# A hybrid decoder trunk on one core: decay matrices from spread loads issued by GpSimd, the delta rule's made once and stored, convolutions in another place in memory

## The chip, the core and the metric

The kernel runs on one core of a Trainium2 chip. The core has TensorE (PE, matrix products, with a separate weight load that overlaps them), VectorE (DVE), ScalarE (ACT), GpSimd (POOL) and SyncE (SP). Each works off its own queue in order; semaphores hold one engine until another is done. DMAs can be issued from the queues of SP, ACT and POOL. On chip are SBUF (128 partitions) and PSUM (banks of 128 partitions x 512 float32, into which PE writes).

The metric is the time of one execution in microseconds (us), the median of several runs. Before the change it is 2346.28 us (three runs, 2346.13 to 2346.67).

## What is computed

Two layers of a trunk with 512 tokens of width 1024, all in float32. In each layer, one projection of the normalised input feeds three branches: an SSD branch (Mamba-2), latent attention (MLA), and a gated delta rule (GDN). Their outputs are gated, summed, projected, and followed by a feed-forward part. The change concerns the decay matrices of two branches. From the reference:

```python
# SSD: 2 groups of 8 heads, chunks of 128 tokens
A_cum = jnp.cumsum(A, axis=-1)
L = jnp.exp(jnp.where(tril, A_cum[..., :, None] - A_cum[..., None, :], -jnp.inf))
CB = jnp.einsum('bclgn,bcsgn->bcgls', Cc, Bc)
y_diag = jnp.einsum('bcgls,bgecls,bcsgep->bclgep', CB, L, X)
# delta rule: 8 heads
g = jnp.cumsum(chunks(g), axis=-1)
decay = jnp.exp(jnp.where(incl, g[..., :, None] - g[..., None, :], -jnp.inf))
a_mat = jnp.where(strict, jnp.einsum('bhcld,bhcmd->bhclm', kb, k) * decay, 0.0)
qk = jnp.where(incl, jnp.einsum('bhcld,bhcmd->bhclm', q, k) * decay, 0.0)
```

So for each head and each block of 128 tokens a matrix exp(c[l] - c[s]) is needed, where c is the running sum of the log decay in the block. There are 16 + 8 = 24 heads and 4 blocks (the reference takes the delta rule in chunks of 64, the kernel in blocks of 128; the output is mathematically the same). The delta rule uses its matrix twice: for the triangular matrix of keys against keys (`a_mat`), and for queries against keys (`qk`). Where l is before s the difference is positive; the kernel clips it at 0 before the exponential, and a mask takes that part away later.

## The kernel before

The kernel is written in a tile language: tiles come from pools, a tag names a set of buffers that its tiles take in turn, and a planner puts the instructions of each engine into an order at build time and sets the semaphores. The order in the source is the priority. So PE's queue holds matmuls of later parts of the source between those of a part that waits. Products in float32 accuracy are made of three products of split operands (`mm3`, L185): a weight tile `raw` is split into `hi` (ACT, L159) and `lo` (DVE, L160); four such pairs are kept (`wp`, 4 buffers of `whi` and `wlo`), and raw weights arrive by SP's DMAs (L166) into two buffers.

The order in each layer:

1. Small projections (64 rotary columns and the 32 columns of step sizes), then the query latent `cq`, the key latent `ck` (`latent`, L510), then four passes of two attention heads (L565 to L687). The pool `ml` holds the tiles of this part, the split latents (`cqh`, `cql`, `ckh`, `ckl`) among them. `step_sizes` (L402) runs after the first pass: it makes the log decays `g24` (128 tokens x 4 blocks x 24 heads), their sums by three matmuls with fixed matrices (`incl`, `gt`, `ones`, L431), and the exponentials of these (`dec`, L433).
2. `ml` is closed (L688) and the pool `br` for the other two branches is opened in the same memory (L709). Its tiles wait for the readers of what lay there.
3. `ssd_group(0)` (L1061): convolutions (`conv_silu`, L692: one ACT instruction and three DVE instructions into an accumulator `cva`, then a SiLU) on B, C (tiles `ft`) and X, the projection z, then four steps, one for each block of tokens t (L745). In each step two decay tiles `eE` of four heads (128 x 4 x 128) are made, multiplied by the masked product of C and B (L755), and used by PE as the left operand in eight products (L760).
4. Two of four parts of the attention's output projection (`out_proj`, L493), `ssd_group(1)`, and the other two parts.
5. `gdn_matrix` for each of two units of four heads (L812): keys, their products, and the triangular matrix `nt` with the decay tile (L845), written to memory (L849); `gdn_blocks` and `gdn_inverse` invert it between the rows of the SSD branch's output projection.
6. `gdn_unit` for the two units (L949): queries, values, z, then four steps with a decay tile each (L988 to L996, the product L1025), a power on POOL in each step (`rsq`, L269), then the branch's output projection.
7. Output projection, feed-forward.

How a decay tile is made before the change: `cum_rows` (L448), called once per layer in group 0 after z (L740), multiplies `g24`, laid out in 128 rows, with `incl` (four matmuls, L462), splits the result into high and low parts and builds from it, with constant selectors `sel` and `ind`, a left operand `W` and a right operand `M` (L464 to L476). `seg_exp` (L481) then takes the rows of four heads with `sel` (DVE, L484), makes all four difference matrices by one matmul of 128 x 512 into a PSUM bank (PE, L486), clips (ACT, L488) and takes the exponential (ACT, L489). It is called 16 times in the SSD groups, 8 times in `gdn_matrix` and 8 times in `gdn_unit`: 32 times per layer, 64 in all. The PSUM pool of these (`sm`) has three banks; `eE` has two buffers.

POOL does the powers (L271, L831, L961) and some memsets; no DMA is issued from its queue.

Of the kernel before, what the change touches and what calls it, by code (L numbers as in the profile page):

```python
# [29 lines left out]
NBLK = 6  # L30
# [6 lines left out]
def shape_constants():  # L37
# [7 lines left out]
    bmask = (k // 32 == np.arange(4)[None, :])  # L45
    r32 = k % 32
    sel = (r32 < 24) & (r32 // 4 == np.arange(6)[None, :])
    ind = (r32 < 24) & (r32 % 4 == np.arange(4)[None, :])
    pad = np.zeros((P, P - 14))
# [5 lines left out]
    mats = [ident, incl, gt, ones, nstrict, bmask, sel, ind, pad, neg, full, invc, sgn]  # L55
# [4 lines left out]
def hybrid_kernel(ctx, tc, a, out, depth=2, taps=None):  # L60
# [4 lines left out]
    def mk(pl, shape, dt, tag, bufs=None):  # L65
        return pl.tile(shape, dt, tag=tag, name=f"{tag}_{next(uid)}", bufs=bufs)
# [30 lines left out]
    def sm_bank():  # L97
        return mk(ps_sm, [P, 512], F32, "sm")
# [4 lines left out]
    ct = mk(cst, [P, NBLK * P + 80], F32, "ct")  # L103
# [6 lines left out]
    bmask, sel, ind = (ct[:, 5 * P + i : 5 * P + j] for i, j in ((0, 4), (4, 10), (10, 14)))  # L110
# [249 lines left out]
    for ly in range(depth):  # L360
# [40 lines left out]

        def step_sizes():  # L402
# [43 lines left out]
            return dec, ndec, beta, dtq, dsk, g24  # L446

        def cum_rows(pl):  # L448

            g4 = mk(pl, [P, T, 4, 32], F32, "wk0")
            pool.memset(g4.rearrange("p t a n -> p (t a n)"), 0.0)
            g2 = g24.unsqueeze(2).to_broadcast([P, T, 2, 24])
            dve.tensor_copy(g4[:, :, 0:2, 0:24], g2)
            dve.tensor_scalar(g4[:, :, 2:4, 0:24], g2, -1.0, None, ALU.mult)
            ps = sm_bank()  # L460
            for t in range(T):
                pe.matmul(ps[:, t * P : (t + 1) * P], g4[:, t].rearrange("p a n -> p (a n)"), incl, start=True, stop=True)  # L462
            hi = mk(pl, [P, S], F32R, "wk1")
            act.copy(hi, ps)  # L464
            lo = mk(pl, [P, S], F32R, "wk2")
            dve.tensor_tensor(lo, ps, f32(hi), ALU.subtract)
            W = mk(pl, [P, T, P], F32R, "cw")
            M = mk(pl, [P, T, 4, P], F32R, "cm")
            dve.tensor_copy(W[:64].rearrange("p t m -> p (t m)"), ones[:64, 0:1].to_broadcast([64, S]))
            i4 = ind.unsqueeze(2).to_broadcast([P, 4, P])  # L470
            for q, x in ((0, hi), (32, lo)):
                act.copy(W[64 + q : 96 + q].rearrange("p t m -> p (t m)"), f32(x[64 + q : 96 + q]))
                for t in range(T):
                    dve.tensor_tensor(M[q : q + 32, t], bc_mid(f32(x[q : q + 32, t * P : (t + 1) * P]), 4), i4[q : q + 32], ALU.mult)
            for t in range(T):
                act.copy(M[64:, t], i4[64:])  # L476
            return W, M

        cum = []

        def seg_exp(pl, o, t, h0):  # L481

            w = mk(pl, [P, P], F32R, "sg", 2)
            dve.tensor_scalar(w, f32(cum[0][:, t]), sel[:, h0 // 4 : h0 // 4 + 1], None, ALU.mult)  # L484
            ps = sm_bank()
            pe.matmul(ps, w, cum[1][:, t].rearrange("p i l -> p (i l)"), start=True, stop=True)  # L486
            of = o.rearrange("p i l -> p (i l)")
            act.activation(of, ps, AF.Relu, scale=-1.0)  # L488
            act.activation(of, of, AF.Exp, scale=-1.0)  # L489
# [20 lines left out]
        def latent(tok, width, gi, nm):  # L510
# [10 lines left out]
            hs, ls = hilo_tags(ml, nm, nk)  # L521
# [9 lines left out]
        cqh, cql = latent(cq_tok, 512, g_q, "cq")  # L531
        ckh, ckl = latent(ck_tok, 256, g_kv, "ck")
# [32 lines left out]
        for hp in range(4):  # L565
# [120 lines left out]
            if hp == 0:  # L686
                dec, ndec, beta, dtq, dsk, g24 = step_sizes()  # L687
# [4 lines left out]
        def conv_silu(pl, ps, taps_, bias, o):  # L692

            acc = mk(pl, [P, S], F32, "cva", 2)
# [17 lines left out]
        def ssd_group(g, yh, yl):  # L712
# [3 lines left out]
            bt = mk(br, [P, S], F32, "ft", 6)  # L716
            ctl = mk(br, [P, S], F32, "ft", 6)
            btok = mk(br, [P, T, P], F32, "kt", 2)

            def conv(ps, c, o):  # L720
                conv_silu(br, ps, [sconv(j, c) for j in range(4)], col(sconv_b + c), o)
# [17 lines left out]
            if g == 0:  # L739
                cum[:] = cum_rows(br)  # L740
# [61 lines left out]
        def gconv_silu(ps, c, o):  # L802
            conv_silu(br, ps, [gconv(j, c) for j in range(4)], None, o)

        def key_tiles(c0):
# [4 lines left out]
            return res  # L810

        def gdn_matrix(u):  # L812
# [136 lines left out]
        def gdn_unit(u, kT, ork, cc, cd, Yt, yh, yl):  # L949
# [35 lines left out]
            for t in range(T):  # L985
                tok = slice(t * P, (t + 1) * P)
                Y = Yt[:, t]
                e = mk(br, [P, 4, P], F32, "eE", 2)  # L988
                seg_exp(br, e, t, hd0)
# [320 lines left out]
```

## Time and profile before

| | |
|---|---|
| median of three runs | 2346.28 us (2346.13 to 2346.67) |
| the profiled execution's own time | 2345.51 us |
| its span, first to last instruction | 2343.7 us |
| granted clock of PE, mean | 0.999 |
| bytes read from and written to device memory | 200.50 MB, 7.34 MB |
| decay matmuls (L486) | 64 |

The profile is of one execution. PE is the matmul side of TensorE, PEld its weight load. A line such as L486 is a line of the kernel before. A group of the profile reads: line, engine, operation, output tile <- input tiles, shape, count, then busy time in us and the mean of one in ns, then the idle time of that engine just before these instructions and what ended most of it. Matmuls are pipelined, so the duration of one is longer than the distance to the next. The chain of waits is followed back from the last instruction to what released each; its rows give a start, a duration and the instruction, and where PE splits a product into several instructions, each is counted.

### The profile page before, as it was taken

What the parts mean: (1) busy time and instruction counts of PE and PEld (TensorE: products, weight loads), DVE (VectorE), ACT (ScalarE), POOL (GpSimd) and SP (SyncE); (2) the same over time, 40 slices, a digit from 0 to 9 for tenths busy, and PEclk for the clock granted to TensorE, in tenths of its full rate; (3) what the DMA queues carried; (4) which work ended last, traced back from release to release, by engine and by line L of the source; (5) the groups of instructions that cost most, each with busy time, mean ns of one, the idle gap of its engine ahead of it and who ended that gap; (6) DMA issues with size and microseconds to landing.
All of it is one profiled execution on the core that took longest, in us unless ns stands there. A gap on an engine that the chain in (4) does not pass through costs nothing.

```text
span 2343.7 us, 32132 instructions
## 1 busy us (share of the span) xinstructions
PE 2310.1 (99%) x12004; PEld 1898.8 (81%) x12004; DVE 1608.3 (69%) x3186; ACT 1153.3 (49%) x2303; POOL 58.3 (2%) x76
## 2 busy tenths in 40 slices
PE   8999999999999999999999999999999999999998
PEld 7787788888887888888888887888887878888886
DVE  6776857775665458767767776667756645677668
ACT  6665434533544345544656553444335534555545
POOL 0000000000000000000000000000000000000000
PEclk9999999999999999999999999999999999999999
DMA  4222222252222442233132222223422124332231
GB/s 137 86 72 66 71 90 72 77 149 73 72 66 70 144 153 101 72 125 117 44 102 79 73 73 72 90 72 99 118 81 72 59 77 156 132 114 102 90 108 45
DMA packets 194173, 215.16 MB, mean 92 GB/s; under 512 B 32353, under 2 KB 153697, under 8 KB 194017
## 3 DMA queue, kind: packets, MB, share of 16 engines
q1 hardware_dynamic: 190496, 207.87, 27.9%
q10 hardware_dynamic: 3520, 5.25, 0.9%
q8 instruction: 94, 1.54, 0.3%
q14 instruction: 63, 0.51, 0.1%
HBM read 200.50 MB, written 7.34 MB: 89 GB/s over the span
## 4 chain that ended last, share of the span: by engine, by line
PE 90%; DVE 5%; ACT 1%; DMA 1%; POOL 1%; issue 1%; SPq 0%; DVEq 0%; POOLq 0%; ACTq 0%
PE acc L187 23%; PE acc L188 23%; PE acc L189 23%; PE sm L187 2%; PE sm L188 2%; PE sm L189 2%; PE sm L760 1%; DVE wlo L160 1%; PE sm L664 1%; PE yt L188 1%; PE sm L1025 1%; PE yt L187 1%; PE yt L189 1%; PE sm L486 1%; PE sm L1006 1%
## 5 line engine op out<-in xcount | busy, mean ns | idle before, releaser
L160 DVE TENSOR_TENSOR wlo<-wraw,whi 128x512 fp32r<-128x512 f32 x552 | 378.1, 688 | 399.7 <-ACT whi L159 389.8
L159 ACT CAST whi<-wraw 128x512 fp32r<-128x512 f32 x552 | 341.9, 621 | 621.0 <-PE acc L188 408.1
L187 PE MATMUL acc<-xh,whi 128*128 128x512 f32 (+1 forms) x1184 | 462.1, 391 | 0.0
L188 PE MATMUL acc<-xl,whi 128*128 128x512 f32 (+1 forms) x1184 | 459.4, 388 | 0.0
L189 PE MATMUL acc<-xh,wlo 128*128 128x512 f32 (+1 forms) x1184 | 459.0, 388 | 0.0
L188 PEld LDWEIGHTS acc<-xl,whi 128*128 128x128 f32 x1184 | 223.0, 188 | 42.3 <-issue 1.0
L189 PEld LDWEIGHTS acc<-xh,wlo 128*128 128x128 f32 x1184 | 222.9, 188 | 42.1 <-issue 0.5
L187 PEld LDWEIGHTS acc<-xh,whi 128*128 128x128 f32 x1184 | 222.8, 189 | 41.7 <-issue 0.5
L187 PE MATMUL acc<-yh,whi 128*128 128x512 f32 x384 | 153.0, 402 | 0.0
L188 PE MATMUL acc<-yl,whi 128*128 128x512 f32 x384 | 152.4, 397 | 0.0
L189 PE MATMUL acc<-yh,wlo 128*128 128x512 f32 x384 | 151.3, 394 | 0.0
L189 PE MATMUL acc<-whi,xl 128*128 128x512 f32 (+1 forms) x384 | 143.8, 375 | 0.0
L187 PE MATMUL acc<-whi,xh 128*128 128x512 f32 (+1 forms) x384 | 143.6, 376 | 0.0
L188 PE MATMUL acc<-wlo,xh 128*128 128x512 f32 (+1 forms) x384 | 143.2, 373 | 0.0
L701 DVE SCALAR_TENSOR_TENSOR cva<-acc,pc,cva 128x511 f32<-128x511 f32 (+2 forms) x168 | 120.2, 743 | 16.8 <-ACT cva L697 9.5
L159 ACT CAST whi<-wr 128x512 fp32r<-128x512 f32 x128 | 79.5, 621 | 68.2 <-PE acc L189 31.9
L189 PE MATMUL acc<-whi,yl 128*128 128x512 f32 x256 | 99.7, 389 | 0.0
L187 PE MATMUL acc<-whi,yh 128*128 128x512 f32 x256 | 99.7, 389 | 0.0
L188 PE MATMUL acc<-wlo,yh 128*128 128x512 f32 x256 | 99.6, 389 | 0.0
L160 DVE TENSOR_TENSOR wlo<-wr,whi 128x512 fp32r<-128x512 f32 x128 | 85.9, 686 | 12.5 <-ACT whi L159 11.7
L187 PEld LDWEIGHTS acc<-yh,whi 128*128 128x128 f32 x384 | 71.6, 188 | 16.8 <-ACT yh L266 2.3
L188 PEld LDWEIGHTS acc<-yl,whi 128*128 128x128 f32 x384 | 72.2, 188 | 16.0 <-issue 1.9
(413 smaller groups left out, 4603.1 us busy)
## 6 DMA issues: line engine op xcount, KB each, us to landing
wraw<-in_w_in_dram SPq DMA_DIRECT2D x148, 512.0 KB, 3.4
wraw<-in_w_up_dram SPq DMA_DIRECT2D x64, 512.0 KB, 3.6
wr<-in_w_down_dram SPq DMA_DIRECT2D x32, 1024.0 KB, 5.0
wraw<-in_w_mla_out_dram SPq DMA_DIRECT2D x16, 512.0 KB, 3.3
wraw<-in_w_ssd_out_dram SPq DMA_DIRECT2D x16, 512.0 KB, 3.4
wraw<-in_w_gdn_out_dram SPq DMA_DIRECT2D x16, 512.0 KB, 3.3
wraw<-in_w_out_dram SPq DMA_DIRECT2D x16, 512.0 KB, 3.6
wraw<-in_mla_w_uq_dram SPq DMA_DIRECT2D x16, 384.0 KB, 3.2
```

The source lines that it names most:

```text
L159: act.copy(hi, raw)
L160: dve.tensor_tensor(lo, raw, f32(hi), ALU.subtract)
L187: pe.matmul(o, ah, bh, start=start, stop=False, skip_group_check=more)
L188: pe.matmul(o, ah, bl, start=False, stop=False, skip_group_check=more)
L189: pe.matmul(o, al, bh, start=False, stop=stop, skip_group_check=more)
L486: pe.matmul(ps, w, cum[1][:, t].rearrange("p i l -> p (i l)"), start=True, stop=True)
L664: pe.transpose(ps[:, n : n + P], pn[t][:, kb * P : (kb + 1) * P], ident)
L701: dve.scalar_tensor_tensor(acc[:, d:], ps[:, : S - d], taps_[3 - d], acc[:, d:], ALU.mult, ALU.add)
L760: pe.matmul(py[:, h * 64 : (h + 1) * 64], e2[h // 4][:, h % 4, :], xd[:, h * 64 : (h + 1) * 64], start=True, stop=True)
L1006: pe.matmul(pw[:, h * P : (h + 1) * P], Y[:, h, :], r[:, h * P : (h + 1) * P], start=True, stop=True)
L1025: pe.matmul(po[:, h * P : (h + 1) * P], pt_[:, h, :], vn[:, h * P : (h + 1) * P], start=True, stop=True)
```

## The change

- The running sums are taken from the first of the three matmuls that `step_sizes` makes anyway (with `incl`): DVE copies 96 columns to a tile `cum`, PE transposes it, ACT copies the result, and SP's queue stores the rows to device memory (`d_c`: 4 blocks x 24 heads x 128 tokens).
- `seg_exp` becomes: a DMA issued from POOL's queue loads the rows of four heads and spreads them to all 128 partitions (2 KB to each, 256 KB); four ACT instructions, one for each head, subtract a column of `cum` and clip; one ACT instruction takes the exponential. No matmul, no DVE instruction and no PSUM bank is used.
- `cum_rows`, its tiles (`cw`, `cm`, `sg`, and its use of `wk0` to `wk2`) and the constants `bmask`, `sel`, `ind` go.
- The delta rule's eight decay tiles are made once, in a new function `gdn_decays` that is called right after `ssd_group(0)`, and stored by POOL's queue to device memory (`d_e`, 256 KB each). `gdn_matrix` and `gdn_unit` load them back by POOL's queue. So decay tiles are made 24 times per layer (16 + 8) and loaded back 16 times.
- `eE` has four buffers.
- The key latent's split tiles (`ckh`, `ckl`) move from the pool `ml` to `lp`, which stays open. The convolutions' accumulators take the place of `ckl0` and `ckl1` (before: two buffers `cva` in `br`, shared with `out_proj`), and the first group's B and C the place of `ckh0` and `ckh1`.
- The scratch memory for software-issued DMAs is set to 8192 bytes.

```diff
-NBLK = 6
+NBLK = 5
...
-    mats = [ident, incl, gt, ones, nstrict, bmask, sel, ind, pad, neg, full, invc, sgn]
+    mats = [ident, incl, gt, ones, nstrict, neg, full, invc, sgn]
...
+        cum = mk(sp, [P, T, 24], F32, "cum")
+        d_c = mk(dr, [T, 24 * P], F32, "d_c", 2)
...
+            dve.tensor_copy(cum.rearrange("p t n -> p (t n)"), ps[:, :96])
+            pc_ = sm_bank()
+            pe.transpose(pc_[:96, :P], cum.rearrange("p t n -> p (t n)"), ident)
+            rows = mk(ml, [96, P], F32, "crow")
+            act.copy(rows, pc_[:96, :P])
+            sync.dma_start(d_c.rearrange("t (n l) -> (t n) l", l=P), rows)
...
-        def cum_rows(pl):
...
-        def seg_exp(pl, o, t, h0):
-
-            w = mk(pl, [P, P], F32R, "sg", 2)
-            dve.tensor_scalar(w, f32(cum[0][:, t]), sel[:, h0 // 4 : h0 // 4 + 1], None, ALU.mult)
-            ps = sm_bank()
-            pe.matmul(ps, w, cum[1][:, t].rearrange("p i l -> p (i l)"), start=True, stop=True)
+        def seg_exp(o, t, h0):
+
             of = o.rearrange("p i l -> p (i l)")
-            act.activation(of, ps, AF.Relu, scale=-1.0)
+            pool.dma_start(of, d_c[t, h0 * P : (h0 + 4) * P].partition_broadcast(P))
+            for i in range(4):
+                act.activation(o[:, i], o[:, i], AF.Relu, scale=-1.0, bias=cum[:, t, h0 + i : h0 + i + 1])
             act.activation(of, of, AF.Exp, scale=-1.0)
...
-        cqh, cql = latent(cq_tok, 512, g_q, "cq")
-        ckh, ckl = latent(ck_tok, 256, g_kv, "ck")
+        cqh, cql = latent(ml, cq_tok, 512, g_q, "cq")
+        ckh, ckl = latent(lp, ck_tok, 256, g_kv, "ck")
...
-            acc = mk(pl, [P, S], F32, "cva", 2)
+            acc = mk(lp, [P, S], F32, f"ckl{next(convs) % 2}")
...
-            bt = mk(br, [P, S], F32, "ft", 6)
-            ctl = mk(br, [P, S], F32, "ft", 6)
+            bt, ctl = (mk(br, [P, S], F32, "ft", 6) if g else mk(lp, [P, S], F32, f"ckh{i}") for i in range(2))
...
-            if g == 0:
-                cum[:] = cum_rows(br)
...
-                e2 = [mk(br, [P, 4, P], F32, "eE", 2) for _ in range(2)]
+                e2 = [mk(br, [P, 4, P], F32, "eE", 4) for _ in range(2)]
                 for q in range(2):
-                    seg_exp(br, e2[q], t, h0 + 4 * q)
+                    seg_exp(e2[q], t, h0 + 4 * q)
...
+        def gdn_decays():
+
+            for u in range(2):
+                for t in range(T):
+                    e = mk(br, [P, 4, P], F32, "eE", 4)
+                    seg_exp(e, t, 16 + 4 * u)
+                    pool.dma_start(d_e[u, t], e)
...
-                e = mk(br, [P, 4, P], F32, "eE", 2)
-                seg_exp(br, e, t, hd0)
+                e = mk(br, [P, 4, P], F32, "eE", 4)
+                pool.dma_start(e, d_e[u, t])
...
+        d_e = mk(dr, [2, T, P, 4, P], F32, "d_e", 2)
         ssd_group(0, *ys)
+        gdn_decays()
         out_proj(a["w_mla_out"][ly], 1, *y_mla, br, (0, 1))
...
-    nc = bacc.Bacc("TRN2", target_bir_lowering=False, num_devices=1)
+    nc = bacc.Bacc("TRN2", target_bir_lowering=False, num_devices=1, dynamic_dma_scratch_size=8192)
```

The replaced call of `seg_exp` by a load stands in two places, `gdn_matrix` and `gdn_unit`.

More of the change, by code (lines that the diff above doesn't have):

```diff
@@ L445, in step_sizes @@
             tap("beta", beta)
[L446 to L486 removed]
+            return dec, ndec, beta, dtq, dsk
+        def seg_exp(o, t, h0):
             of = o.rearrange("p i l -> p (i l)")
[L488 removed]
+            pool.dma_start(of, d_c[t, h0 * P : (h0 + 4) * P].partition_broadcast(P))
+            for i in range(4):
+                act.activation(o[:, i], o[:, i], AF.Relu, scale=-1.0, bias=cum[:, t, h0 + i : h0 + i + 1])
             act.activation(of, of, AF.Exp, scale=-1.0)
@@ L507, in out_proj, with latent @@
                         dve.tensor_tensor(mixed[d], mixed[d], tg[j], ALU.add)
-        def latent(tok, width, gi, nm):
+        def latent(pl, tok, width, gi, nm):
             nk = width // P
@@ L802, in gconv_silu @@
         def gconv_silu(ps, c, o):
-            conv_silu(br, ps, [gconv(j, c) for j in range(4)], None, o)
+            conv_silu(ps, [gconv(j, c) for j in range(4)], None, o)
         def key_tiles(c0):
@@ L987, in gdn_unit @@
                 Y = Yt[:, t]
[L988 to L989 removed]
+                e = mk(br, [P, 4, P], F32, "eE", 4)
+                pool.dma_start(e, d_e[u, t])
                 pg = sm_bank()
```

17 lines of the change are left out of this document (6 added, 11 removed).

## The prediction

> **What bounds the kernel now.** I read the page's busy times first, then the shares of the chain of waits, then the table by stage, and last the groups of single lines.
>
> ```profile
> span 2343.7 us, 32132 instructions
> PE 2310.1 (99%) x12004; PEld 1898.8 (81%) x12004; DVE 1608.3 (69%) x3186; ACT 1153.3 (49%) x2303; POOL 58.3 (2%) x76
> ...
> PE 90%; DVE 5%; ACT 1%; DMA 1%; POOL 1%; issue 1%; SPq 0%; DVEq 0%; POOLq 0%; ACTq 0%
> ```
>
> TensorE (PE) is busy 99% of the span and makes up 90% of the chain that ended last; only 33.6 us of the span (2343.7 - 2310.1) has no matmul in it. GpSimd (POOL) does almost nothing. But a busy PE may be one that waits with a matmul open, so I looked at the stages that the change touches. In layer 0 they are: group 0 of the SSD branch, the time from there to group 1, group 1, the delta rule's matrices, the delta rule's two units. Columns: stretch, its length, then busy time of PE, weight load, DVE, ACT, POOL, granted clock, DMA share, GB/s.
>
> ```profile
> 236.00:284.00 48.00, 47.13 (x234) 37.12 (x232) 42.66 (x79) 22.22 (x44) 1.02 (x1) 1.00 0.19 57
> 284.00:358.00 74.00, 73.67 (x335) 60.30 (x336) 40.72 (x63) 30.23 (x50) 0.00 (x0) 1.00 0.30 92
> 358.00:395.00 37.00, 37.00 (x187) 29.17 (x186) 30.50 (x59) 16.90 (x35) 1.01 (x1) 1.00 0.19 58
> 432.00:470.00 38.00, 37.13 (x179) 30.31 (x178) 34.14 (x118) 20.53 (x36) 5.31 (x6) 1.00 0.30 86
> 600.00:732.00 132.00, 129.73 (x667) 105.27 (x666) 91.12 (x242) 67.90 (x176) 10.07 (x9) 1.00 0.19 60
> ```
>
> PE stands still for 0.87 us in group 0, for nothing in group 1, for 0.87 us at the matrices and 2.27 us in the units. The clock is full. VectorE (DVE) is the second engine everywhere: 89% in group 0 (42.66 of 48) and 90% at the matrices. ScalarE (ACT) is half idle. So a matmul that is taken out should shorten the kernel by the distance between two matmuls, as long as DVE's chain does not become the pace.
>
> **What is removed from PE.** The decay matrices are made by one matmul each (L486), on rows that `cum_rows` makes by four matmuls in each layer (L462).
>
> ```profile
> L486 PE MATMUL sm<-cm,sg 128*128 128x512 f32 x64 | 26.5, 445 | 0.6 <-DVE sg L484 0.6
> ...
> 170.33 0.39 PE L187 MATMUL acc<-xh,whi 128*128 128x512 f32 x1
> ...
> 171.01 0.39 PE L187 MATMUL acc<-xh,whi 128*128 128x512 f32 x1
> ...
> 237.08 0.89 PE sm L462 x8
> ...
> 1396.78 0.89 PE sm L462 x8
> ```
>
> The 445 ns of an L486 is its latency in a pipeline. Its price is the distance of starts: the two L187 rows, from a dense stretch, are three matmuls of the same width apart, 0.68 us, so 0.227 us each. 64 x 0.227 = 14.5 us. The chain has L462 with 0.89 us in each layer, 1.8 us together. Added on PE is one 96-column transpose per layer; eight narrow matmuls take 0.89, so 0.11 each, 0.2 us. Net: 14.5 + 1.8 - 0.2 = 16.1 us.
>
> Not all of it must count. 16 of the 64 L486 stand in the units (4 steps, 2 units, 2 layers), where PE already has its longest waits. If the recurrence sets the pace there, those 16 x 0.227 = 3.6 us come back as waiting. Between 0 and 3.6 I take the middle, 1.8: PE is idle in that stage for only 2% of the time, but the chain passes through GpSimd's and DVE's small steps there. Gain so far: 16.1 - 1.8 = 14.3 us.
>
> **DVE and ACT.** All are off the bound; these are their sums.
>
> ```profile
> L484 DVE TENSOR_SCALAR sg<-cw,ct 128x128 fp32r<-128x128 f32 x64 | 18.3, 300 | 10.0 <-PE sm L486 10.0
> L474 DVE TENSOR_TENSOR cm<-wk,ct 32x512 fp32r<-32x512 f32 x16 | 10.2, 675 | 0.1
> ...
> L489 ACT ACTIVATE eE<-eE 128x512 f32<-128x512 f32 x64 | 39.2, 630 | 0.7
> L488 ACT ACTIVATE eE<-sm 128x512 f32<-128x512 f32 x64 | 37.0, 595 | 45.5 <-PE sm L486 34.2 <-DVE tok L845 11.3
> ...
> L476 ACT CAST cm<-ct 64x512 fp32r<-64x512 f32 x8 | 4.5, 612 | 0.1
> ...
> 609.47 1.14 ACT L1013 ACTIVATE wk<-sm,gcd 128x128 f32<-128x128 f32 x4 [0.73 <-DVE wk L1008]
> ```
>
> DVE loses L484 and L474, 28.5 us, and gains one small copy per layer. DVE also loses a wait of 10.0 us for L486. That helps group 0 most: two L484 out of each step and eight L474 ahead of the first. I count no gain for it, because PE is full there; the bounds are 0 and, in both layers, the still time of the first three and the fourth rows above, 2 x (0.87 + 0.33 + 0 + 0.87) = 4.1 us. On ACT a clip becomes four instructions of 128x128 with a column as bias. The nearest row is L1013, four of 128x128 with a column as scale in 1.14 us. Matrices are made 48 times and no longer 64, for the delta rule's are stored and loaded twice. Out go 37.0 + 39.2 + 4.5 = 80.7 us, in come 48 x (1.14 + 0.63) = 85.0 us: 4 us more on an engine that is idle half the time. Where it is dense, behind group 0, eight matrices are added: 8 x 1.77 = 14.2 us on 30.23 of 74. It fits.
>
> **The DMAs.** New are 48 spread loads, 16 stores and 32 loads back, all 256 KB and all on POOL's queue, and two small stores of the sums on SP's. No POOL DMA runs in the trace, so its price has to be bounded from other queues.
>
> ```profile
> L831 POOL TENSOR_TENSOR gork<-gss,phalf 128x8 f32<-128x8 f32 x4 | 6.6, 1638 | 130.9 <-DVE gss L829 130.9
> ...
> qh<-in_positions_dram SPq DMA_DIRECT2D x1, 256.0 KB, 4.9
> ...
> wk<-d_x SPq DMA_DIRECT2D x4, 256.0 KB, 5.0
> ...
> L166 SPq DMA_DIRECT2D wraw<-in_w_in_dram x148: 367/368/433, 4.5 to 1927.5; - x148
> ...
> L876 SPq DMA_DIRECT2D wk<-d_x x4: 371/1468/3038, 511.9 to 1672.0; - x4
> ```
>
> The load of the positions has exactly the new form, one 2 KB row spread over 128 partitions: 4.9 us from issue to landing. POOL's time for an issue lies between SP's usual 0.37 us and the longest issue of an L876, 3.04 us; I take 1.6, POOL's longest own calculation (L831), since the engine does such work in software steps. 96 x 1.6 = 154 us on an engine with 2285 us to spare. By bytes, 96 x 0.26 = 25 MB on 215: a twelfth more on queues that are busy 28%.
>
> Whether a load is late depends on the steps. Rows: the first products with a decay matrix in group 0, the last ones there, the first ones of group 1.
>
> ```profile
> 249.45 1.01 PE sm L760 x8
> ...
> 275.99 1.73 PE sm L760 x16
> ...
> 282.74 1.03 POOL srs L271
> ...
> 360.13 1.08 PE sm L760 x8
> ...
> L433 ACT ACTIVATE dec<-sm x2: 417/417/417, 105.0 to 1266.0; 128x288 f32<-128x288 f32 x2
> ```
>
> The sums are there at L433, 105 us, 144 us ahead of 249. SP's new store stands in front of weight loads in its queue and waits for one ACT copy at that time; I count nothing, and 2 x 0.6 us if that copy is behind another. Steps 0 and 1 of a group find their four buffers filled early. Between groups 20 issues (8 loads, 8 stores, 4 loads) have 360 - 276 = 84 us: hidden up to 4.2 us each. Steps 2 and 3 are the tight ones: a buffer is free after the products of the step two before, and a step is (275.99 - 249.45) / 3 = 8.8 us, so two steps less the products and the mask give about 14 us. Needed are two issues, 4.9 us, and two clips with exponentials, 3.5 us. Hidden up to (14 - 8.4) / 2 = 2.8 us per issue. With 1.6 nothing is exposed; with 3.04 it is 2 x 0.24 us for each of 8 pairs of loads (2 steps, 2 groups, 2 layers), 4 us.
>
> Behind a waiting load stand POOL's powers (L271). The group's is at 282.74 and its result is used a whole projection later. In unit 0 a load for unit 1 is free to go at the same step's last product, and the power comes after the copy, DVE and ACT work that follow that product. Behind a waiting clip stand ACT's weight casts.
>
> ```profile
> L159 ACT CAST whi<-wraw 128x512 fp32r<-128x512 f32 x552 | 341.9, 621 | 621.0 <-PE acc L188 408.1 <-PE acc L189 122.3 <-PE sm L188 25.0
> ...
> L895 ACT COPY tok<-wk 32x512 f32<-32x512 f32 x4 | 2.5, 617 | 5.5 <-DMA wk<-d_x 5.5
> ```
>
> The casts sit idle because PE has not yet freed a buffer (408.1 of 621.0 us): they run ahead. A pair of buffers feeds 12 matmuls, 2.7 us; three pairs in reserve cover 8.2 us.
>
> [...]
>
> **Convolution in the latent's place.** The first convolutions no longer need memory that attention frees.
>
> ```profile
> 180.00:190.00 10.00, 10.00 (x60) 7.95 (x59) 6.47 (x18) 5.00 (x14) 0.53 (x1) 1.00 0.17 52
> 190.00:200.00 10.00, 9.99 (x52) 8.06 (x51) 7.43 (x14) 7.52 (x15) 0.00 (x0) 1.00 0.16 52
> ```
>
> PE does not stop at that passage (10.00 and 9.99 of 10), so it is worth nothing; its cover is PE's other queued matmuls, and with less of these it could be worth the few tenths that stand idle there. Smaller constants and scratch cost no time.
>
> **Sum.** The profiled span is 2343.7 us and its run 2345.51, against a median of 2346.28: 2.6 us lie between span and median. 2343.7 - 14.3 + 2.6 = 2332.0 us. With the bounds (0 or 3.6 lost in the units, 4.1 won from still time, 4 + 1.2 lost to issues and SP) the forecast's own range is 2326 to 2339.
>
> **Rivals.**
> (a) The engines behind PE set the pace. For: DVE at 89 to 90% in group 0 and the matrices. Against: PE idles under 1 us there, and DVE is relieved too. Then the 32 matmuls in the groups and the 16 in the units give nothing, 48 x 0.227 = 10.9, of which 1.8 is counted: 2332 + 9.1 = 2341.
> (b) The loads of steps 2 and 3 come late and hold ACT, whose order is fixed, and so PE's products behind it: the one place where the change adds a short wait. For: L895 is such a wait of ACT for a load from memory, 5.5 us in two layers, 2.75 each. Against: 5.6 us of slack for each pair. At 2.75 for each of the 8 pairs: 22 us, 2354. It decides from 14.3 / 8 = 1.8 us per pair. If an issue held POOL for the whole 5.0 us, a pair would lose 2 x 2.2 us, 35 us, 2367.
> (c) More than the matmuls is won: three PSUM banks no longer shared with the decay matrices, ACT no longer waiting 34.2 us for L486 and DVE 10.0 us. For: these rows. Against: no idle PE to win it from. If the still time of the touched stages, units too, 2 x 4.34 = 8.7 us, went: 2332 - 8.7 = 2323.
>
> **From this to the numbers.** Forecast 0.58, (a) 0.12, (b) 0.20, (c) 0.10. This kernel's runs spread by 0.02%, and I call 0.2%, 4.7 us, the least that can be told from no change: faster is under 2341.6, slower over 2351.0. Faster: forecast, (c), and half of (a), 0.74. Same: the rest of (a) and 0.04 of (b), 0.10. Slower: 0.16. The range goes from 2320, under (c), to 2354, (b) at L895's price; outside are about 0.10 above and 0.03 below.
>
> **What will show it.** Right: PE's count of 128x512 matmuls falls by 64 and L462 is gone, while PE stays at 99%; the clips wait for no load in steps 2 and 3; POOL's issues take under 2.8 us. Wrong: ACT's new clip line with waits for loads of 2 us and more, followed by PE waiting in the L760 line; POOL's power in the units starting late behind a load; or PE's share falling below 98% at 236 to 284 and 600 to 732 with DVE nearly full, which would be (a).

## The result and the profile after

The changed kernel takes 2352.71 us (median of 19 runs, 2344.45 to 2358.88), the kernel before 2347.03 on the same chip (19 runs, 2346.13 to 2349.86): a ratio of 1.0024, 95% interval [1.0017, 1.0031]. It is 5.7 us slower, where 14.3 us less was forecast. The runs of before lie within 4 us, those of after within 14. The profiled execution of after is the slowest of them, 2358.88 us, so the traces differ by more than the medians: 13.4 us of span. Line numbers are those of each kernel, so the same code stands at a lower number in after.

The head of the page of after, and its chain of waits:

```profile
span 2357.1 us, 32210 instructions
...
PE 2305.1 (98%) x11926; PEld 1898.6 (81%) x11926; DVE 1582.6 (67%) x3100; ACT 1159.7 (49%) x2403; POOL 112.2 (5%) x170
...
PE 80%; issue 6%; DVE 6%; DMA 4%; ACT 2%; POOL 1%; SPq 0%; ACTq 0%; POOLq 0%; DVEq 0%
```

The matmuls are gone (78 records fewer), yet PE is busy only 5.0 us less, and the time without a matmul rose from 33.6 to 52.0 us. In the chain DMA rose from 1% to 4%, and "issue", time in which an engine waits for nothing that the profile shows, from 1% to 6%. Where PE stands still is shown by the waits of PE, and why by the waits of ACT (waiting tile and line, what it waited for, us in total, times, longest):

```profile
PE sm L730 <- DVE eE L725: 10.0, 6, 2.1
PE sm L879 <- DMA wk<-d_x: 5.9, 2, 3.7
...
ACT eE L457 <- DMA eE<-d_c: 39.7, 20, 5.0
```

L730 are the products with a decay matrix in the ssd groups (L760 before), L725 the mask on that matrix, L879 the first products of the delta rule's inverse (L901 before, where this wait was 0.9 us). Before has no wait over 0.3 us at these products or at the matmuls that make their matrices. The same shows by stage, in columns as in the prediction's table:

```profile
232.00:280.00 48.00, 43.15 (x215) 33.62 (x214) 34.40 (x60) 28.47 (x72) 9.44 (x17) 1.00 0.43 132
280.00:354.00 74.00, 73.99 (x336) 60.80 (x335) 37.12 (x55) 39.07 (x78) 4.81 (x9) 1.00 0.44 129
354.00:395.00 41.00, 38.91 (x190) 30.50 (x189) 30.87 (x53) 18.78 (x44) 4.68 (x9) 0.96 0.37 115
...
600.00:740.00 140.00, 136.75 (x704) 112.04 (x703) 92.48 (x240) 61.87 (x164) 13.41 (x13) 1.00 0.26 73
```

In group 0, PE is idle for 4.85 us of 48 (0.87 before), though DVE fell from 89% to 72% and ACT is at 59%: no engine is full, so something is late. In group 1 the granted clock is 0.96 and no longer full. What is late in group 0 is seen in the timelines of POOL, ACT, DVE and PE (start, duration, engine, line; in brackets the idle time ahead and what ended it):

```profile
240.90 0.55 POOL L455 DMA_DIRECT2D eE<-d_c  x1 [43.31 <-DVE wlo L154]
242.65 0.55 POOL L455 DMA_DIRECT2D eE<-d_c  x1 [1.20 <-ACT st L747]
...
248.10 0.55 POOL L455 DMA_DIRECT2D eE<-d_c  x1 [0.34 <-ACT eE L458]
...
244.58 0.40 ACT L457 ACTIVATE eE<-eE,cum 128x128 f32<-128x128 f32 x1 [2.67 <-DMA eE<-d_c]
...
248.71 0.63 ACT L458 ACTIVATE eE<-eE 128x512 f32<-128x512 f32 x1
...
253.35 0.40 ACT L457 ACTIVATE eE<-eE,cum 128x128 f32<-128x128 f32 x1 [0.59 <-DMA eE<-d_c]
...
254.81 0.69 DVE L154 TENSOR_TENSOR wlo<-wraw,whi 128x512 fp32r<-128x512 f32 x1 [2.40 <-ACT whi L153]
...
256.25 0.96 PE L730 MATMUL sm<-wk,eE 128*128 128x64 f32 x7 [1.88 <-DVE eE L725]
```

POOL starts the loads of step 2 at 240.90 and 242.65, when the products of step 0 have freed their buffers. ACT, in its fixed order, stands at the clips until they land. But step 2's matrix is finished in time: its second exponential (248.71) ends at 249.34, and PE comes to its products at 254.37 (256.25 less the 1.88 of waiting). What is late is its mask, and the chain of waits ahead of these products shows by what:

```profile
248.10 5.14 DMA eE<-d_c
...
253.35 0.07 ACT eE L457
...
253.66 0.61 ACT eE L458
254.27 0.52 ACT whi L153
...
254.81 0.04 DVE wlo L154
...
255.42 0.70 DVE eE L725
...
256.25 1.09 PE sm L730 x8
```

The load of 248.10 belongs to step 3. ACT stands at its clip; behind the clip, in ACT's order, stands a weight cast (L153); for that cast DVE stands 2.40 us at the weight's low part (L154); and behind L154, in DVE's order, stands the mask of step 2. At step 3's products, where PE waits another 1.88 us until 267.40, the same chain begins at the first loads for the delta rule, issued at 257.86 and 258.75. Right ahead of the mask of each of the six waits at L730 stands an L154 that waited 1.2 to 2.6 us for its cast. In group 1, where no spread load follows those of step 3, step 3 has no such wait.

At the inverse two things are seen, the windows of PE's wait and of what follows, and the first products:

```profile
516.00:519.00 3.00, 0.00 (x0) 0.00 (x0) 0.61 (x2) 0.62 (x1) 0.00 (x0) 0.98 0.85 181
519.00:529.00 10.00, 9.55 (x148) 7.35 (x151) 2.88 (x5) 4.60 (x8) 0.00 (x0) 0.50 0.67 131
529.00:540.00 11.00, 11.00 (x240) 9.01 (x238) 4.98 (x8) 6.56 (x12) 0.00 (x0) 1.00 0.19 51
...
519.45 1.92 PE L879 MATMUL sm<-wk,tok 32*32 32x32 f32 x64 [3.68 <-DMA wk<-d_x]
```

PE waits 3.68 us for the blocks, and then the granted clock (the number behind POOL's) is 0.50 for 10 us. The 64 products took 1.20 us before, here 1.92. The trace has six such stretches while PE works: 3.4 us at 378.9, 1423.4, 1443.9 and 1546.3, 10.2 us at 518.9, 13.7 us at 1686.2. Each begins 2.7 to 4.2 us after the start of a wait of PE of 1.5 to 3.7 us. Before has none.

### The profile page after: what moved, and what is told of

Same layout as the page of the kernel before. It is cut to its first block, busy times and chain, and to the rows that moved or that the text cites. A ratio compares the mean times of both kernels' runs of the same rounds, so it can differ in the third digit from the quotient of the medians.

```text
span 2357.1 us, 32210 instructions
## 1 busy us (share of the span) xinstructions
PE 2305.1 (98%) x11926; PEld 1898.6 (81%) x11926; DVE 1582.6 (67%) x3100; ACT 1159.7 (49%) x2403; POOL 112.2 (5%) x170
## 3 DMA queue, kind: packets, MB, share of 16 engines
q0 software_dynamic: 7680, 25.17, 3.5%
## 4 chain that ended last, share of the span: by engine, by line
PE 80%; issue 6%; DVE 6%; DMA 4%; ACT 2%; POOL 1%; SPq 0%; ACTq 0%; POOLq 0%; DVEq 0%
PE acc L181 20%; PE acc L182 20%; PE acc L183 20%; PE sm L182 2%; PE sm L181 2%; PE sm L183 2%; DMA eE<-d_c 1%; DVE wlo L154 1%; DVE tok L846 1%; PE sm L730 1%; DMA mix<-mix 1%; DVE gQ L845 1%; PE sm L633 1%; PE yt L182 1%; PE sm L1003 1%
## 5 line engine op out<-in xcount | busy, mean ns | idle before, releaser
L154 DVE TENSOR_TENSOR wlo<-wraw,whi 128x512 fp32r<-128x512 f32 x552 | 378.4, 689 | 443.2 <-ACT whi L153 433.8
L153 ACT CAST whi<-wraw 128x512 fp32r<-128x512 f32 x552 | 341.4, 621 | 611.5 <-PE acc L182 371.4
L674 DVE SCALAR_TENSOR_TENSOR ckl<-acc,pc,ckl 128x511 f32<-128x511 f32 (+2 forms) x168 | 120.4, 743 | 16.8 <-ACT ckl L670 8.2
L153 ACT CAST whi<-wr 128x512 fp32r<-128x512 f32 x128 | 79.5, 621 | 68.2 <-PE acc L183 32.0
L154 DVE TENSOR_TENSOR wlo<-wr,whi 128x512 fp32r<-128x512 f32 x128 | 85.9, 687 | 12.3 <-ACT whi L153 11.7
L457 ACT ACTIVATE eE<-eE,cum 128x128 f32<-128x128 f32 x192 | 64.2, 391 | 46.7 <-DMA eE<-d_c 39.7
```

The costliest lines, as they stand in the source:

```text
L153: act.copy(hi, raw)
L154: dve.tensor_tensor(lo, raw, f32(hi), ALU.subtract)
L457: act.activation(o[:, i], o[:, i], AF.Relu, scale=-1.0, bias=cum[:, t, h0 + i : h0 + i + 1])
L674: dve.scalar_tensor_tensor(acc[:, d:], ps[:, : S - d], taps_[3 - d], acc[:, d:], ALU.mult, ALU.add)
```

## The experiments

Theory A: the loss is made of (i) loads of steps 2 and 3 that start only when products free a buffer, on which ACT stands, (ii) the wait at the inverse, and (iii) half clock behind such waits. The rivals are named with each run. Every kernel was timed beside the kernel before on its chip.

**Eight buffers.** On the changed kernel:

```diff
-                e2 = [mk(br, [P, 4, P], F32, "eE", 4) for _ in range(2)]
+                e2 = [mk(br, [P, 4, P], F32, "eE", 8) for _ in range(2)]
```

(and the same in the three other places that take an eE)

> The changed kernel with eight buffers for decay tiles (eE) where it has four, so that the loads of a group's last two steps need not wait for the products of its first two. Theory A (these loads come late, hold ACT, and PE waits): ACT's waits for the loads in the clip line fall from 39.7 us to under 10, the six waits of PE ahead of the L730 products (1.88, 1.88, 2.09, 1.51, 0.52, 2.08 us, together 10.0) nearly vanish, and so do the half-clock stretches that follow them (378.9, 1423.4, 1443.9, 1546.3 us, 3.4 us each, costing half of that, 6.8 us): 2352.7 - 10 - 6.8 = 2336, between 2333 and 2342. Theory B (the time is lost at the inverse and in the units, the loads are absorbed): 2350 to 2354.

Measured: 2357.59 us (2351.22 to 2359.79), ratio 1.0041 [1.0028, 1.0054]. Slower than both kernels at the median, and outside both theories' ranges. Waits of ACT and PE, the last exponential of group 0, and DVE ahead of step 2's mask:

```profile
ACT eE L457 <- DMA eE<-d_c: 18.8, 13, 3.9
...
PE sm L730 <- DVE eE L725: 6.8, 3, 2.5
PE yt L763 <- DVE tok L758: 5.8, 2, 3.6
...
230.45 0.63 ACT L458 ACTIVATE eE<-eE 128x512 f32<-128x512 f32 x1
...
255.13 0.69 DVE L154 TENSOR_TENSOR wlo<-wraw,whi 128x512 fp32r<-128x512 f32 x1 [2.47 <-ACT whi L153]
```

All eight loads of group 0 now start ahead of it, and its eight matrices are ready by 231.1 us, save for the mask. PE still waits 1.95 and 2.34 us at the products of steps 2 and 3. As soon as group 0's first products free a buffer, POOL takes it for the delta rule's loads, whose clips stand between group 0's other work on ACT. ACT waits for those landings in the same place, and the cast, L154 and the mask stand behind it as before. So what PE pays for is not a load that is late for its own products. More buffers in the same ring only let the next user in earlier.

**The inverse two rows of matmuls later.**

```diff
-            if next(rows) >= 23 and steps:
+            if next(rows) >= 25 and steps:
                 steps.pop(0)()
...
+        for step in steps:
+            step()
```

> The changed kernel with the first step of the inverse put behind two more rows of matmuls of the output projection (row 25 and not 23), the two steps left over after it; PE then has 2.7 us more to do while the block inverses come back from memory. Theory A (removing matmuls ahead of this place made PE reach it too early, the wait dropped the clock, and the clock costs more than the wait): the waits of 3.68 and 2.23 us ahead of L879 shrink to about 1.0 and 0, the half-clock stretches of 10.2 and 13.7 us behind them vanish: 2352.7 - 4.9 - up to 12 = 2336 to 2343. Theory B (small products are bound by their issue, so the half clock costs nothing there): 2347 to 2349. Theory C (the wait only moves to the first unit, which needs the inverse): 2351 to 2354.

Measured: 2346.16 us (2342.42 to 2350.68, 11 runs), ratio 0.9998 [0.9989, 1.0006]; 6.5 us less than the changed kernel. In its trace the wait of 3.68 us at the inverse is 0.35 us, that of layer 1 is gone, and so is the half clock at both. The waits at L730 stay (11.7 us). The gain lies between A's range and B's: the waits and the half clock at the inverse went as A said, but they gave less. Between the first Gram products (keys against keys) of the delta rule's second unit and the inverse stand 272 matmuls of the projections in before, 273 in after, 285 here. Four decay matmuls are gone from that stretch, so PE comes to the inverse 0.8 us sooner in after than in before; the data of the blocks land 2.7 us later in layer 0 and 0.8 us in layer 1. The 12 matmuls of cover, 2.7 us, hide most of it.

**Both.**

> Both edits of the two runs before. If the two losses are separate and both real, the gains add: 2352.7 - 16 - 12 = about 2325, with PE idle back to about 19 us, no half-clock stretch inside the span, and the whole gain of the removed matmuls (16 us) shown; range 2322 to 2332. If one of them is only moved about, 2335 to 2345.

Measured: 2353.44 us (2348.6 to 2355.42), ratio 1.0027 [1.0015, 1.0039]. The gains do not add, and the time lies outside both ranges. The inverse's waits are gone, those of the eight buffers stay (2.43, 2.25 and 2.96 us in group 0, 7.74 us behind it in layer 1).

**The wait at the inverse filled.** 28 products that nothing uses, ahead of the first products of the inverse:

```diff
+                if u == 0:
+                    pw = y_bank()
+                    for i in range(28):
+                        pe.matmul(pw[:, :P], ident, ident, start=True, stop=True)
```

> The changed kernel with 28 products of a constant with itself in each layer (about 6 us of PE), whose result nobody reads, put in PE's queue right ahead of the first products of the inverse, that is into PE's wait there. Work is added and none taken away. Theory A (the half clock behind this wait is the dearer part): the half-clock stretches of 10.2 and 13.7 us vanish, and the kernel gets faster by up to 12 us less the few tenths by which the filling overshoots: 2341 to 2348. Theory B (the half clock is only a sign of the wait and costs no time there): 2353 to 2358.

Measured: 2354.99 us (2353.76 to 2357.02), ratio 1.0037 [1.0024, 1.0049]. PE has neither the wait nor the half clock there (two stretches remain, in layer 1's groups), but nothing was won. The filling takes 6.4 us in each layer, 12.8 together, where the waits were 5.9, and it also moved the inverse ahead by 12 matmuls in PE's order. Without the filling PE is busy for 2293.3 us (2306.1 - 12.8), 11.8 less than in after. So the half clock has a price, but the four stretches of after outside the inverse have become two, and this run does not settle the price at the inverse alone.

**Tiles of their own for the loads.** This takes (i) away at its root: the load no longer needs the products' buffer.

```diff
-            pool.dma_start(of, d_c[t, h0 * P : (h0 + 4) * P].partition_broadcast(P))
+            r = mk(br, [P, 4, P], F32, "eR", 4)
+            pool.dma_start(r.rearrange("p i l -> p (i l)"), d_c[t, h0 * P : (h0 + 4) * P].partition_broadcast(P))
             for i in range(4):
-                act.activation(o[:, i], o[:, i], AF.Relu, scale=-1.0, bias=cum[:, t, h0 + i : h0 + i + 1])
+                act.activation(o[:, i], r[:, i], AF.Relu, scale=-1.0, bias=cum[:, t, h0 + i : h0 + i + 1])
```

> The changed kernel, with the spread load landing in four tiles of its own (eR) and the clips reading them and writing the decay matrix (eE, four as before). A load then waits only for the clips of the load four before it, not for the products. Theory A (the steps 2 and 3 of an ssd group are late because their loads are issued when products free the buffer, and ScalarE, which works in order, stands at the clip until they land): ScalarE's waits at the clips on the load fall from 39.7 us to under 15 us; PE's waits of 1.5 to 2.1 us at the products of group 0 and 1 (10.0 us in all) and the half clock behind them go; time 2338 to 2348, the inverse's waits stay. Rival B (it is the clip work itself or VectorE's products that are late): PE's waits in the groups stay within 3 us of their sum, time 2350 to 2356.

Measured: 2333.74 us (2330.44 to 2335.68), ratio 0.9939 [0.9926, 0.9951]. Its windows at the groups, and what its clips (now L458) still wait for:

```profile
232.00:280.00 48.00, 47.75 (x236) 37.52 (x235) 35.47 (x61) 36.87 (x94) 12.82 (x22) 1.00 0.51 151
...
354.00:395.00 41.00, 41.00 (x205) 32.38 (x204) 32.12 (x59) 18.11 (x43) 3.18 (x5) 1.00 0.29 91
...
ACT eE L458 <- PE sm L731: 5.6, 10, 0.6
...
ACT eE L458 <- DMA d_e<-eE: 4.3, 4, 1.2
```

ACT has no wait for a spread load left; in group 0 of layer 0 the L154 ahead of the masks of steps 2 and 3 waits 0.27 and 0.28 us for its cast, and not 2.40 and 2.29; PE is full in both groups and the clock too. ACT works more in that window than in after (36.87 us against 28.47), so the amount of its work was not the cause. 19 us came off the changed kernel, more than A gave. At the inverse, layer 1 still waits 2.17 us, with half clock for 10.2 us behind it.

**Own tiles and the later inverse.**

> Both edits: the spread loads in tiles of their own, and the inverse's steps begun two rows later in the out-projection. Theory A (these two places hold all of the loss): the sum of PE's waits over 0.3 us falls to that of the kernel before (19 us) or under, half clock at most once; time 2332 to 2342, faster than both kernels. Rival B (a lost wait comes back at the next place, as the eight buffers did): 2344 to 2352.

Measured: 2328.97 us (2327.73 to 2331.75), ratio 0.9921 [0.9908, 0.9935], faster than both kernels, and a little under A's range. Its page:

```profile
span 2330.0 us, 32201 instructions
...
PE 2291.2 (98%) x11926; PEld 1889.2 (81%) x11926; DVE 1582.2 (68%) x3100; ACT 1161.8 (50%) x2403; POOL 112.5 (5%) x170
```

No half clock is left while PE works. This kernel has the same matmuls as after, so the three pages can be set against each other:

| kernel | span | PE busy | without a matmul |
|---|---|---|---|
| before | 2343.7 | 2310.1 | 33.6 |
| after | 2357.1 | 2305.1 | 52.0 |
| own tiles, later inverse | 2330.0 | 2291.2 | 38.8 |

From before to after: 18.9 us less for the matmuls (2310.1 - 2291.2), 13.9 us more for the same matmuls at a lower clock (2305.1 - 2291.2), 18.4 us more of waiting (52.0 - 33.6). That is the +13.4 us of the spans. That the 13.9 us are the clock is borne out by the runs between: with the same matmuls PE is busy for 2294.3 us with 6.8 us of half clock (the later inverse) and for 2297.5 with 10.2 (the convolutions put back, below), against 2291.2 with none and 2305.1 with 37.5.

**The kernel before, inverse two rows earlier.** Nothing of the change is in it:

```diff
-            if next(rows) >= 23 and steps:
+            if next(rows) >= 21 and steps:
```

> The kernel before, nothing of the change in it, with the inverse's steps begun two rows of matmuls earlier in the out-projection (21 in place of 23), so that PE comes to them sooner. Theory A (a wait of PE of some 2 us or more is followed by half clock): PE waits 2 to 6 us in each layer at the inverse's first products, a stretch of half clock of 3.4 us or longer follows in at least one layer, and the time rises by the waits and by half of the stretch: 2350 to 2358. Rival B (the half clock comes from something in the changed kernel, its loads or ScalarE's work, not from the waits): no half clock; the time rises by the waits alone or less, 2347 to 2351.

Measured: 2356.93 us (2355.14 to 2358.07), ratio 1.0039 [1.0026, 1.0051]. The first products stayed where they were (272 matmuls ahead of them), but the next step moved up, and PE waits there. Its waits, windows and the products behind:

```profile
PE sm L917 <- issue: 4.5, 2, 2.3
...
523.50:525.50 2.00, 0.00 (x0) 0.00 (x0) 0.21 (x1) 1.15 (x2) 0.00 (x0) 1.00 0.01 3
527.50:530.90 3.40, 3.40 (x16) 2.80 (x14) 1.39 (x2) 1.11 (x2) 0.00 (x0) 0.50 0.03 2
1688.00:1698.00 10.00, 8.78 (x48) 6.81 (x48) 2.07 (x3) 2.30 (x4) 0.00 (x0) 0.50 0.17 48
...
528.30 0.79 PE L187 MATMUL acc<-xh,whi 128*128 128x512 f32 x1
528.89 0.63 PE L188 MATMUL acc<-xl,whi 128*128 128x512 f32 x1
```

A wait of 2.17 us, and 2 us after its end matmuls take 0.63 us and not 0.39; in layer 1, 2.31 us bring 10.2 us of half clock. PE is busy 6.8 us longer than before with the same matmuls and idle 3.4 us longer, together the 10.2 us of the spans. So the half clock follows waits in a kernel that has nothing of the change; rival B falls.

**Storing alone.** The kernel before, whose matmul-made matrices for the delta rule are made once, stored and loaded back:

```diff
+        def gdn_decays():
+            for u in range(2):
+                for t in range(T):
+                    e = mk(br, [P, 4, P], F32, "eE", 2)
+                    seg_exp(br, e, t, 16 + 4 * u)
+                    pool.dma_start(d_e[u, t], e)
...
-                seg_exp(br, e, t, hd0)
+                pool.dma_start(e, d_e[u, t])
...
+        d_e = mk(dr, [2, T, P, 4, P], F32, "d_e", 2)
         ssd_group(0, *ys)
+        gdn_decays()
```

(the replaced call stands in `gdn_matrix` and in `gdn_unit`)

> The kernel before, with one part of the change alone: the delta rule's matrices, still made by matmuls, are made once behind the first ssd group, stored, and loaded back twice; eE keeps two buffers. 16 of the 64 matmuls of 0.227 us go, 3.6 us. Theory A (storing costs nothing by itself; the loss is at the ssd groups' loads and at the inverse reached early): 2341 to 2346, no half clock. Rival B (the stores and loads of 256 KB hold the two buffers and with them VectorE): 2347 to 2353, with new waits of PE behind the first group or at the matrices.

Measured: 2362.93 us (2360.22 to 2366.08), ratio 1.0066 [1.0053, 1.0078]; slower than either theory said. Waits of PE and DVE, and DVE's timeline at the matrices:

```profile
PE sm L909 <- DMA wk<-d_x: 7.9, 2, 4.3
...
DVE tok L853 <- DMA eE<-d_e: 7.7, 6, 1.6
...
458.77 2.19 DVE L853 SCALAR_TENSOR_TENSOR tok<-eE,gcc,wk 128x128 f32<-128x128 f32 x8 [0.89 <-DMA eE<-d_e]
...
470.64 1.14 DVE L853 SCALAR_TENSOR_TENSOR tok<-eE,gcc,wk 128x128 f32<-128x128 f32 x4 [1.42 <-DMA eE<-d_e]
473.03 1.14 DVE L853 SCALAR_TENSOR_TENSOR tok<-eE,gcc,wk 128x128 f32<-128x128 f32 x4 [1.25 <-DMA eE<-d_e]
```

With two buffers DVE waits for the loads back at the matrices, the blocks' data come late, and PE pays at the inverse, with two stretches of 13.7 us of half clock. Rival B names the mechanism; the place where it is paid is a stage later.

**Storing alone, inverse later.**

> The kernel before with the delta rule's matrices stored (as in e7_stored_only) and the inverse's steps begun two rows later (25 in place of 23). Theory A (all that storing costs is that PE comes to the inverse too early, with the half clock behind that wait): PE's waits of 3.54 and 4.32 us at the inverse's first products fall to under 1 us, no half clock while PE works, and the time is that of the kernel before less the 16 matmuls: 2341 to 2346. Rival B (the stores and loads cost elsewhere too): 2348 to 2356, with the waits at the inverse gone.

Measured: 2356.64 us (2353.84 to 2359.70), ratio 1.0039 [1.0025, 1.0053]. Both theories missed: the waits did not go.

```profile
PE sm L909 <- DMA wk<-d_x: 6.7, 2, 3.5
```

Only five more matmuls came ahead of the inverse here (285 against 280), and in layer 0 the store of the blocks went out 1.1 us later as well. What went is half clock: two stretches of 3.4 us, where there were two of 13.7. Storing with two buffers is a loss at both places of the inverse that were tried; storing matmul-made matrices with four buffers wasn't tried.

**The convolutions put back**, in the kernel of own tiles and later inverse:

```diff
-        ckh, ckl = latent(lp, ck_tok, 256, g_kv, "ck")
+        ckh, ckl = latent(ml, ck_tok, 256, g_kv, "ck")
...
-            acc = mk(lp, [P, S], F32, f"ckl{next(convs) % 2}")
+            acc = mk(pl, [P, S], F32, "cva", 2)
...
-            bt, ctl = (mk(br, [P, S], F32, "ft", 6) if g else mk(lp, [P, S], F32, f"ckh{i}") for i in range(2))
+            bt, ctl = (mk(br, [P, S], F32, "ft", 6) for i in range(2))
```

> The kernel of e6_own_load_buffers_inverse_later with the convolutions and the key latent put back where the kernel before had them (buffers cva and ft). Theory A (the move only makes room and costs nothing): 2327 to 2332, within 2 us of that kernel. Rival B (the move gives part of the gain, or takes part of it back): more than 3 us from 2329, to either side.

Measured: 2339.78 us (2334.85 to 2341.39), ratio 0.9962 [0.9950, 0.9975]: 10.8 us more than with the move (10.2 when each is set against the kernel before on its own chip), as rival B has it. The same window in the kernel with the move (first row) and, in the second fence, without it:

```profile
196.00:212.00 16.00, 15.96 (x85) 12.52 (x84) 12.32 (x23) 9.26 (x21) 2.35 (x4) 1.00 0.33 99
```

```profile
196.00:212.00 16.00, 14.03 (x61) 10.99 (x60) 11.90 (x19) 11.48 (x26) 1.33 (x3) 0.89 0.51 158
...
PE acc L181 <- DVE cva L675: 3.9, 2, 2.0
```

Without the move PE waits 1.96 us in each layer for an accumulator that the first convolutions hold, and half clock follows both times. A third stretch of 3.4 us, at 149.0, stands inside attention, behind waits of 0.87 and 0.70 us, ahead of these convolutions; it is part of the 10.8 us in the profiled execution, and what the move has to do with it is open. With the move the first two convolutions' sums are done by 185 us, inside attention. Before had no such wait with the same placing; the trace without the move has the first clips on ACT in this window (from 202 us), but that they are the reason wasn't tried.

## Why the prediction was wrong

**The matmuls: right.** 16.1 us were reckoned for PE, 18.9 us less of PE's busy time were found where the clock is full. A gain of the forecast's size, 14.3 us, is reached once the rest is out of the way: 13.6 us with own tiles (2347.35 to 2333.74), 18.4 with the later inverse as well. The move of the convolutions is in both; of the 18.4 without it 8.2 are left (2347.99 to 2339.78). The 1.8 us taken off for the units came out too: PE's waits at L1006 were 1.3 us before and are 3.5 us at the same code in after and with own tiles.

**The issues on POOL and the landing: right, and on the safe side.** 1.6 us an issue were taken, with bounds 0.37 and 3.04. Here are the loads' issues by line, and the landings:

```profile
L455 POOL DMA_DIRECT2D eE<-d_c x48: 538/548/719, 195.2 to 1535.9; - x48
...
eE<-d_c POOLq DMA_DIRECT2D x48, 256.0 KB, 4.2
...
eE<-d_e POOLq DMA_DIRECT2D x32, 256.0 KB, 3.7
```

An issue of a spread load takes 0.55 us, and at most 0.72. That it costs POOL as much as one of its own calculations, 1.6 us, was the author's assumption; the page names the kind of POOL's queue software_dynamic (7680 packets, 25.17 MB), but no issue took half of the 1.6 us. The landings, 4.2 us at the median for the spread loads and 3.7 for the loads back, are under the 4.9 us reckoned with. The new DMAs add 25 MB to 215, which is 12% and not a twelfth; nothing hung on that.

**The slack of steps 2 and 3: the step that failed.** The reckoning itself held. The prediction gave a load about 14 us from the freed buffer to the products, and 8.4 us that it needs. In after the first products of step 0 end at 240.38 and PE comes to those of step 2 at 254.37, 14.0 us later; from the issue at 240.90 to the end of step 2's second exponential at 249.34 pass 8.4 us. What failed is the use of it: "5.6 us of slack for each pair" was counted up to the pair's own products and set against rival (b). ACT comes to the clips long before that and stands there as long as a load is out, 39.7 us in 20 places. What stands behind the clip was counted as casts that "run ahead" and cover 8.2 us of PE's weights. Behind the cast on DVE stands its low part, and behind that a mask that PE needs at once; of this order the prediction has nothing. So a load for the next step, or for the delta rule, holds up a matrix that is itself ready. The eight buffers show it, where all of group 0's own matrices were ready more than 20 us ahead and the waits stayed; own tiles, with which a load no longer waits for products, took the waits away. That the chain runs over DVE's order is read from the traces; a kernel with only that order changed wasn't tried.

Rival (b) was thus right in its place and in what is held, ACT and behind it PE's products, and the sign that the prediction names for it (waits of 2 us and more at the clip, then PE waiting at the L760 line) is what the trace shows. Its price was not: the waits at L730 are 10.0 us in 6 places, not 22 in 8. That its 2354 lies close to the measured 2352.71 is luck: the loss is made up of waits at other places and of the clock as well.

**The clock: no term for it.** "The clock is full" was read as a property of the kernel. In before it went with short waits: once PE has begun, at 2.8 us, none is over 1.4 us, and there is no half clock while it works. 13.9 us of the profiled execution, the slowest of its 19 runs, are the half clock behind waits, more than the waits at L730 themselves.

**The inverse: not looked at.** The change puts loads back into the stage ahead of it and nothing in the sum had a wait there. Before waits there for 0.9 us in all, so it has no margin; with PE 0.8 us sooner in each layer and the data of the blocks 2.7 and 0.8 us later this became 5.9 us of waits and the two longest stretches of half clock. Its part is the 6.5 us of the run with the later inverse, or 4.8 with own tiles (2333.74 to 2328.97). What exactly delays the data wasn't taken apart: the small stores of the matrices (d_n) took 4.4 us to land at the median and 2.0 before, the load behind them 5.1 and 4.2, at the time of the units' loads back, which fits with contention but doesn't show it.

**The move of the convolutions: "worth nothing" was wrong.** In before PE doesn't stop at that passage, and a few tenths were allowed for. In the kernel with own tiles and the later inverse the move is worth 10.8 us; that it is the decay work on ACT that makes the difference is not shown.

The table above accounts for the whole difference of the spans; which part of the 13.9 us belongs to which wait was separated only at the inverse, and there not cleanly.

## What to carry to other kernels

A load that lands in time for its own consumer can still be late for an engine that waits for it in its fixed order. So for each new wait list what stands behind it on that engine, and what stands behind that on the next one; here it was two queues away, at the mask of another step. A tile that is loaded by DMA and then turned in place into an operand ties the load to the operand's reader; two tiles free the load, and here that was worth 19 us where four more buffers in the same ring were worth nothing. A wait of an engine that is 99% busy can cost more than its length: in the kernel before with the inverse earlier, two waits of 2.2 and 2.3 us came with 6.8 us of longer matmuls. So look for the places with no margin even where the change does not touch them.

## What was not expected of the hardware

In the trace of after, waits of PE of 1.5 to 3.7 us were followed, 2.7 to 4.2 us after they began, by half clock for 3.41, 10.24 or 13.65 us. In the kernel before with the inverse earlier a wait of 2.17 us was, 4 us after it began, and in the trace without the convolutions' move 3.4 us of half clock stand behind waits of 0.87 and 0.70 us. Not every wait was: two of 1.88 us in group 0 of the changed kernel were not, while 1.51 us at 1419.64 was.

The starts lie on a grid. In the trace of after the other five are 41, 306, 312, 342 and 383 times 3.4133 us, a third of the 10.24 us, behind the first, to within 0.01 us, and the stretches are one, three and four of these long. What makes the grid is not shown. Cut along it, the trace has, from 20 us to PE's last product, three pieces at full clock in which PE stood idle for over 1.7 us (3.08, 2.23 and 1.74), and half clock followed all three. Of seven with 1.1 to 1.7 us it followed three (1.37, 1.31 and 1.18, and not 1.65, 1.45, 1.35 and 1.13), and none with less than 1.0 us. Each of the two waits of 1.88 us falls into two pieces, with 1.65 us and 1.13 us in the larger part. So neither the length of a wait nor its share in one piece settles by itself whether half clock follows.

The half clock also goes with an unsteady time: over the 19 runs of after the span falls by 1.9 us for each 0.001 of mean granted clock (correlation -0.92); they spread over 14 us and those of before over 4.
